# Spreading eight heads' attention tasks over a calendar, float32 sums of squares, one more weight sum by accumulating DMA, and padding tiles, in a one-core encoder layer

## The chip, the cores and the metric

One core of a Trainium2 chip runs the whole kernel as one program. The metric is the device time of one execution in microseconds (us). TensorE (PE) multiplies, VectorE (DVE), ScalarE (ACT) and GpSimd (POOL) do elementwise work, SyncE (SP) and POOL issue DMAs.

## The reference

One residual layer over 512 frames of width 2048. A combined projection gives q, k, v (8 heads of 128), u and v_sgu (1024 each) and two gates (2048 each). Attention is stick-breaking: no softmax, strictly causal.

```python
h = rms_norm(x, g_mix)
q, k, v_sb, u, v_sg, gate_a, gate_b = jnp.split(h @ w_in, splits, axis=-1)
q, k = rms_norm(q, g_q), rms_norm(k, g_k)                    # per head
z = einsum('bhtd,bhsd->bhts', q, k) * 128 ** -0.5
log_keep = where(past, log_sigmoid(-z), 0)
a = where(past, exp(log_sigmoid(z) + tail_sum(log_keep)), 0) # tail: over later s < t
y_a = (a @ v_sb) @ w_oa
y_b = (gelu(u) * (W_s LN(gelu(v_sg)) + b)) @ w_ob            # W_s: 8 groups, 128 x 128
x = x + (sigmoid(gate_a) * y_a + sigmoid(gate_b) * y_b) @ w_out
x = x + square(relu(rms_norm(x, g_ff) @ w_ff1)) @ w_ff2
```

## The kernel before

**Numbers.** Matrix operands are held as two float32r parts, `hi` and `lo` (hi by an ACT cast, lo by a DVE subtraction, `split_to`, L106 to L112), and a product is the sum of two or three float32r matmuls over the parts (`mm3`, L72 to L74).

**Stages.** v and v_sgu are projected by tokens (`by_token`). Then comes the stage that the change touches: a list `order` of 28 *pairs* of 128-column blocks of `w_in` (20 gate pairs, 8 head pairs, where a head's pair is its q and k). Then the projections `ya`, `yb`, `xo`, the hidden layer in pairs too (`w_ff1`), and the last product (`w_ff2`).

**A pair.** `strassen_pair` computes one pair in seven products (Strassen's scheme in Winograd's form) in the sequence `TREE = ("y11", "m7", "m6", "y21", "m5", "m4", "y22")`. PE does 16 matmuls for each (L221 with `hi`, L224 with `lo`; m7 has 24 by `mm3`). Several products run on in one PSUM bank, the *trunk* (named `q`), and after y11, m6 and m5 ACT copies the trunk into another bank (`fork`, L229), from which y21, m4 and y22 go on. The weights of a product are sums of four loaded blocks w11, w12, w21, w22, 512 KB each: `Sums.parts` makes the sum and splits it. In `parts`, "m7" is w11 + w21 (DVE, L181); "m5" is w21 + w22, done by a DMA that POOL issues with `accum_op=ALU.add` (L183); "m6" adds w22 to the m7 sum in the tile `c` (DVE, L185); "y22" adds w12 to `c` (DVE, L187).

**Attention tasks.** When a head's pair is done, `attend(h, act)` returns 18 small tasks, which are put into the queue `behind`; `step()`, called after every product, takes one task from it. A task only records instructions behind that product's. The tasks are, in this order: `square` of q, `of_q`, `square` of k, `of_k`, nothing, `scaled_k`, nothing, `weigh(3)`, `weigh(2)`, `weigh(1)`, `weigh(0)`, `fetch_v`, nothing, `turn(0)`, `turn(1)`, `turn(2)` with `turn(3)`, nothing, `product`. So they fill 18 of the 21 products from one head's pair to the next (`order` has two gate pairs between heads).
- `square` (L525) squares q or k on ACT and splits the squares into hi and lo. `factors` (L532) sums them over the head's 128 dimensions: eight float32r matmuls of 4 columns into `ms`; POOL raises that to the power -1/2 (`r`, L537).
- `of_k` makes two diagonal matrices `dg` of k's factors by eight ACT instructions (L552); `scaled_k` multiplies them by ones on PE (`rows`, L558) and scales k.
- `weigh(tb)` is one block row of the attention: scores `z` on PE, two sigmoids on ACT (`keep` L579, `beta` L580), a masking and a running product on DVE (L581, L584), a masking on POOL (L587), and the product `beta` on DVE (L588).
- `turn(sb)` transposes the finished weights on PE (`aT`, L597) and splits them; `product` multiplies them by v into `o`.

**What sets the order.** The code is recorded in the order above, and then each engine's instruction stream is arranged by the framework's own estimate of times; on the chip each engine goes through its stream strictly in that order, and waits where an operand isn't there.

Of the kernel before, what the change touches and what calls it, by code (L numbers as in the profile page):

```python
# [16 lines left out]
P = 128  # L17
# [18 lines left out]
def tile_hybrid_layer(ctx: ExitStack, tc: tile.TileContext, x, g_mix, w_in, g_q, g_k, ln_g, ln_b,  # L36
# [39 lines left out]
    state = {"load": None, "raw": raws}  # L76
    behind = collections.deque()

    def step():
        if behind:  # L80
            behind.popleft()()

    def flush():
        while behind:
            step()

    def weight(wap, kt, c0, w=W):
# [75 lines left out]
    class Sums:  # L163


        def __init__(self, blocks, tiles, loaded=True):


            self.blocks, self.loaded = blocks, loaded
            self.w11, self.w12, self.w21, self.w22, self.a, self.c = tiles  # L170
            self.take = {"y11": self.w11, "y21": self.w12, "m7": self.a, "m6": self.c, "y22": self.c,
                         "m4": self.w22, "m5": self.w21}
# [6 lines left out]
        def parts(self, name):  # L179
            if name == "m7":  # L180
                nc.vector.tensor_tensor(out=self.a, in0=self.w11, in1=self.w21, op=ALU.add)  # L181
                if self.loaded:
                    state["sum"] = nc.gpsimd.dma_start(out=self.w21, in_=self.blocks[1, 1], accum_op=ALU.add)  # L183
            if name == "m6":
                nc.vector.tensor_tensor(out=self.c, in0=self.a, in1=self.w22, op=ALU.add)  # L185
            if name == "y22":
                nc.vector.tensor_tensor(out=self.c, in0=self.c, in1=self.w12, op=ALU.add)  # L187
            if name == "m5" and not self.loaded:
                nc.vector.tensor_tensor(out=self.w21, in0=self.w21, in1=self.w22, op=ALU.add)
            src = self.take[name]  # L190
            hi, lo = piece("w_hi"), piece("w_lo")
            like = "p (k c) -> p k c"
            hi, lo = (t.rearrange(like, k=src.shape[1]) for t in (hi, lo))
            split_to(hi, lo, src)
            return hi, lo

    def column_sums(wap, c0, loaded=True):

        KH = KT // 2
        c0 = c0 if isinstance(c0, tuple) else (c0, c0 + P)  # L200
        blocks = {(h, c): wap[:, c0[c]:c0[c] + P].rearrange("(k h p) c -> h p k c", p=P, h=2)[h]
                  for h in range(2) for c in range(2)}
        w = Sums(blocks, [state["raw"].tile([P, KH, P], F32, name="w_raw", tag="w_raw") for _ in range(6)],
                 loaded)
        collections.deque(w.loads(), 0)
        return w

# [64 lines left out]
        def __getitem__(self, k):  # L272
            return self.ys[self.name, k]

    def strassen_pair(wap, c0, ys, forks, loaded=True, ready=None):
# [11 lines left out]
        w, first = ready or (column_sums(wap, c0, loaded), None)  # L287
        strassen_columns(w, {name: Late(ys, name) for name in NAMES}, forks, evac, first)
        return act

# [71 lines left out]
    mhalf = const.tile([P, 4], F32, name="mhalf")  # L362
    nc.gpsimd.memset(mhalf, -0.5)

    minus_one = const.tile([P, 4], F32, name="minus_one")
    nc.gpsimd.memset(minus_one, -1.0)
    ones_r = const.tile([P, P], F32R, name="ones_r")
# [146 lines left out]
    def attend(h, act):  # L514
# [5 lines left out]
        def small4(name, dt=F32):  # L520
            return small.tile([P, NTB], dt, name=name, tag=name, bufs=3)

        def square(src):
            t = slot("sq")
            nc.scalar.activation(out=t, in_=src, func=AF.Square)  # L525
            part["sq"] = split(t, "sq")

        def factors():
            m = acc("ms")
            for tb in range(NTB):  # L530
                for i, sq in enumerate(part["sq"]):
                    nc.tensor.matmul(m[:, tb * 4:tb * 4 + 4], lhsT=sq[:, tb * P:(tb + 1) * P], rhs=ones_r[:, :4],  # L532
                                     start=i == 0, stop=i == 1)
            t, f = small4("ms"), small4("r")
            nc.vector.tensor_tensor(out=t, in0=m[:, :16].rearrange("p (b r) -> p b r", r=4)[:, :, 0], in1=eps_x,
                                    op=ALU.add)
            nc.gpsimd.tensor_tensor(out=f, in0=t, in1=mhalf, op=ALU.pow)  # L537
            return f

        def of_q():  # L540
            r[1], r[-1] = factors(), small4("nr")
            nc.gpsimd.tensor_tensor(out=r[-1], in0=r[1], in1=minus_one, op=ALU.mult)
            part["q"] = split(q, "qT")

        def of_k():
            f, f_hi, f_lo = factors(), small4("r_hi", F32R), small4("r_lo")
            nc.vector.tensor_copy(out=f_hi, in_=f)
            nc.vector.tensor_tensor(out=f_lo, in0=f, in1=f32(f_hi), op=ALU.subtract)
            part["dg"] = [slot("dg", F32R) for _ in range(2)]
            for t, x in zip(part["dg"], (f32(f_hi), f_lo)):  # L550
                for tb in range(NTB):
                    nc.scalar.activation(out=t[:, tb * P:(tb + 1) * P], in_=ident, func=AF.Copy,  # L552
                                         scale=x[:, tb:tb + 1])

        def scaled_k():
            rows = acc("rows")
# [47 lines left out]
        def product():  # L604
# [3 lines left out]
            for i, x in enumerate(split(o, "oT")):  # L608
                nc.sync.dma_start(out=held_o[h, i], in_=f32(x))

        return [lambda: square(q), of_q, lambda: square(k), of_k, lambda: None, scaled_k, lambda: None,
                lambda: weigh(3), lambda: weigh(2), lambda: weigh(1), lambda: weigh(0), fetch_v, lambda: None,
                lambda: turn(0), lambda: turn(1), lambda: (turn(2), turn(3)), lambda: None, product]

    wsT, ws, bs = [], [], []
    held_s = dram.tile([6, P, W], F32, name="held_s")
# [83 lines left out]
    opened = []  # L700

    def open_gates():
        w = column_sums(win, US)
        opened.append((w, w.parts(TREE[0])))

    for half in range(2):
# [24 lines left out]

    gate_pairs = [(US + n * P, n, AF.Gelu) for n in range(0, SGW // P, 2)]
    gate_pairs += [(GA + n * P, SGW // P + n, AF.Sigmoid) for n in range(0, 2 * D // P, 2)]
    order = gate_pairs[:2]
    for h in range(HEADS):
        order += [h] + gate_pairs[2 * h + 2:2 * h + 4]
    order += gate_pairs[2 * HEADS + 2:]
    behind.append(moments)
    forks = new_forks(hy["y11", 0])
    oT = []  # L740
# [4 lines left out]
    for i, item in enumerate(order):  # L745
        if i == len(order) - 1:
            with tc.issue_after(state["sum"].ins):
                for h in range(2):
                    fetch_o(h, slots)
        if isinstance(item, int):  # L750
            behind.extend(attend(item, strassen_pair(win, (item * P, SBW + item * P), hy, forks)))
        else:
            c0, n, func = item
            gated(n, strassen_pair(win, c0, hy, forks, ready=opened.pop() if opened else None), func)

    with tc.issue_after(state["sum"].ins):
        for h in range(2, HEADS):
# [333 lines left out]
```

## Time and profile before

| | |
|---|---|
| median of 3 runs | 2515.2 us (2514.13 to 2515.55) |
| the profiled execution | 2515.11 us, of which its span is 2513.4 us |
| PE busy | 2460.3 us of the span |
| DVE, ACT, POOL busy | 1908.5, 1278.4, 434.5 us |
| HBM traffic | 383.29 MB read, 89.65 MB written |

Matmuls overlap in the rows: a 128x512 matmul is shown with 395 ns, and the next begins about 233 ns after it, so the number that counts is the distance between starts. PEclk is the granted clock of TensorE as a share of full speed. In the stage with the 28 pairs (about 180 to 870 us of the span) the tasks of the heads lie between the products.

### The profile page before, as it was taken

How to read it: one execution, taken by the hardware profiler on the slowest of the kernel's cores; microseconds unless marked ns; L12 is line 12 of the kernel's file. 1: busy time of each engine (PE TensorE's matmuls, PEld its weight loads, DVE VectorE, ACT ScalarE, POOL GpSimd, SP SyncE). 2: the span in 40 equal slices, each digit the busy share in tenths (PEclk: the TensorE clock that was granted, in tenths of full speed). 3: DMA queues.
4: the chain of work that ended last, by engine and by line, in shares of the span. 5: the costliest groups of instructions: out<-in, count | busy, mean ns of one | idle time of the engine just before them, and what ended most of it. 6: DMA issues, size and time to landing. Idle time of an engine off the chain costs nothing.

```text
span 2513.4 us, 35343 instructions
## 1 busy us (share of the span) xinstructions
PE 2460.3 (98%) x12920; PEld 2090.3 (83%) x12920; DVE 1908.5 (76%) x2541; ACT 1278.4 (51%) x1931; POOL 434.5 (17%) x556
## 2 busy tenths in 40 slices
PE   9999899999999999999999999999999999999999
PEld 7788788888888878888898888888888878888887
DVE  4567777777777755533689888888888998888887
ACT  5235565655655422322467777767665443333333
POOL 0101120212121332300000000000014334322210
PEclk9999999999999999999999999999999999999999
DMA  5555556555554863433469988888886999866753
GB/s 181 189 150 151 126 130 149 132 137 140 132 137 126 257 227 126 152 126 126 117 160 244 225 235 221 227 230 222 232 273 237 289 306 301 248 213 198 236 173 96
DMA packets 482653, 476.31 MB, mean 190 GB/s; under 512 B 20208, under 2 KB 372528, under 8 KB 482480
## 3 DMA queue, kind: packets, MB, share of 16 engines
q1 hardware_dynamic: 385232, 336.68, 42.2%
q0 software_dynamic: 96960, 136.87, 24.2%
q8 instruction: 101, 1.65, 0.3%
q10 hardware_dynamic: 288, 0.52, 0.1%
q14 instruction: 72, 0.59, 0.1%
HBM read 383.29 MB, written 89.65 MB: 188 GB/s over the span
## 4 chain that ended last, share of the span: by engine, by line
PE 61%; DVE 1%; DMA 0%; issue 0%; ACT 0%; ACTq 0%; DVEq 0%
PE q L72 9%; PE q L73 9%; PE q L74 9%; PE fork L221 7%; PE q L221 7%; PE fork L224 4%; PE q L224 4%; PE xo L74 2%; PE xo L72 2%; PE xo L73 2%; PE yb L73 1%; PE yb L74 1%; PE yb L72 1%; DMA store<-ys 0%; PE f L72 0%; PE f L73 0%
## 5 line engine op out<-in xcount | busy, mean ns | idle before, releaser
L108 ACT CAST w_hi<-w_raw 128x1024 fp32r<-128x1024 f32 (+1 forms) x639 | 669.3, 1048 | 719.8 <-PE q L73 338.4
L109 DVE TENSOR_TENSOR w_lo<-w_raw,w_hi 128x1024 fp32r<-128x1024 f32 (+1 forms) x639 | 780.3, 1222 | 245.9 <-ACT w_hi L108 230.2
L73 PE MATMUL q<-w_lo,ys 128*128 128x512 f32 x896 | 353.9, 395 | 0.7 <-DVE w_lo L109 0.7
L74 PE MATMUL q<-w_hi,ys 128*128 128x512 f32 x896 | 353.8, 395 | 0.0
L221 PE MATMUL q<-ys,w_hi 128*128 128x512 f32 x1192 | 311.1, 398 | 11.3 <-ACT fork L229 11.3
L72 PE MATMUL q<-w_hi,ys 128*128 128x512 f32 x896 | 318.5, 396 | 0.6 <-ACT w_hi L108 0.5
L221 PEld LDWEIGHTS q<-ys,w_hi 128*128 128x128 f32 x1192 | 210.5, 188 | 50.3 <-ACT fork L229 13.0
L221 PE MATMUL fork<-ys,w_hi 128*128 128x512 f32 x968 | 245.6, 395 | 0.0
L183 POOL DMA_DIRECT2D w_raw<-in_w_ff_dram x58 | 80.9, 1394 | 915.0 <-ACT act L282 325.7
L96 DVE TENSOR_TENSOR w_lo<-w_raw,w_hi 128x1024 fp32r<-128x1024 f32 x99 | 124.7, 1259 | 144.4 <-ACT w_hi L94 144.2
L94 ACT CAST w_hi<-w_raw 128x1024 fp32r<-128x1024 f32 x99 | 103.7, 1048 | 238.7 <-issue 84.5
L221 PEld LDWEIGHTS fork<-ys,w_hi 128*128 128x128 f32 x968 | 175.4, 188 | 35.5
L73 PEld LDWEIGHTS q<-w_lo,ys 128*128 128x128 f32 x896 | 167.9, 187 | 42.9 <-DVE w_lo L109 1.5
L72 PEld LDWEIGHTS q<-w_hi,ys 128*128 128x128 f32 x896 | 167.8, 187 | 42.0 <-ACT w_hi L108 0.9
L74 PEld LDWEIGHTS q<-w_hi,ys 128*128 128x128 f32 x896 | 168.1, 188 | 40.9
L224 PEld LDWEIGHTS q<-ys,w_lo 128*128 128x128 f32 x1192 | 162.5, 188 | 13.4
L224 PE MATMUL q<-ys,w_lo 128*128 128x256 f32 x1192 | 165.8, 281 | 0.0
L990 POOL DMA_DIRECT2D ys<-store x224 | 126.1, 588 | 186.0 <-PE q L74 118.6
L224 PEld LDWEIGHTS fork<-ys,w_lo 128*128 128x128 f32 x968 | 131.9, 189 | 11.0
L1033 DVE SCALAR_TENSOR_TENSOR total<-q,plus,total 128x512 f32<-128x512 f32 x180 | 132.5, 744 | 6.6 <-PE q L74 4.8
L224 PE MATMUL fork<-ys,w_lo 128*128 128x256 f32 x968 | 134.2, 281 | 0.0
L72 PE MATMUL q<-ys,w_hi 128*128 128x256 f32 x472 | 133.2, 282 | 0.0
(270 smaller groups left out, 4566.5 us busy)
## 6 DMA issues: line engine op xcount, KB each, us to landing
w_raw<-in_w_ff_dram SPq DMA_DIRECT2D x256, 512.0 KB, 5.6
w_raw<-in_w_in_dram SPq DMA_DIRECT2D x143, 512.0 KB, 4.2
ys<-store POOLq DMA_DIRECT2D x224, 256.0 KB, 6.2
w_raw<-in_w_ff_dram POOLq DMA_DIRECT2D x58, 512.0 KB, 6.7
store<-ys_hi SPq DMA_DIRECT2D x90, 256.0 KB, 4.2
store<-ys_lo SPq DMA_DIRECT2D x90, 256.0 KB, 5.5
w_raw<-in_w_out_dram SPq DMA_DIRECT2D x32, 512.0 KB, 4.0
w_raw<-in_w_in_dram POOLq DMA_DIRECT2D x28, 512.0 KB, 6.3
```

Of the source, the lines that this page charges most:

```text
L72: nc.tensor.matmul(o, lhsT=lh[0], rhs=rh[0], start=start, stop=False, **kw)
L73: nc.tensor.matmul(o, lhsT=lh[0], rhs=rh[1], start=False, stop=False, **kw)
L74: nc.tensor.matmul(o, lhsT=lh[1], rhs=rh[0], start=False, stop=stop, **kw)
L94: nc.scalar.copy(out=hi, in_=raw)
L96: nc.vector.tensor_tensor(out=lo, in0=raw, in1=f32(hi), op=ALU.subtract)
L108: nc.scalar.copy(out=hi, in_=src)
L109: state["lo"] = nc.vector.tensor_tensor(out=lo, in0=src, in1=f32(hi), op=ALU.subtract)
L183: state["sum"] = nc.gpsimd.dma_start(out=self.w21, in_=self.blocks[1, 1], accum_op=ALU.add)
L221: nc.tensor.matmul(o, lhsT=hi[:, k, :], rhs=rhs[name][k], start=name == "y11" and k == 0, stop=False, skip_group_check=True)
L224: nc.tensor.matmul(o[:, :HS], lhsT=lo[:, k, :], rhs=rhs[name][k][:, :HS], start=False, stop=k == KH - 1, skip_group_check=True)
L990: nc.gpsimd.dma_start(out=f32(t), in_=store[f][HELD.index(name), p])
L1033: nc.vector.scalar_tensor_tensor(out=a, in0=o, scalar=part, in1=a, op0=ALU.mult, op1=ALU.add)
```

## The change

1. `attend` no longer returns a list. It puts its tasks into a `calendar`, each at a fixed number of steps after the head's pair: 1, 2, 4, 5, 7, 8, 10, 13, 15, 17, 19, 24, 25, 26 and 30, where before it took 18 steps in a row. `of_k`'s diagonals become two tasks of their own. The next head comes after 21 steps, so a head's last tasks stand among the next head's first.
2. The squares are not split any more: four float32 matmuls instead of eight float32r ones add them up.
3. In the 28 pairs of this stage (`twice=True`) the sum for y22 is made by a second accumulating DMA, issued by POOL behind the split for m6, instead of by DVE.
4. Two tiles of 32 bytes that nothing uses are added, in the pools `const` and `small`. In the built program the 2048-byte slots then begin at a multiple of 128 bytes (before: 64 bytes past one) and the weight pieces too (before: 96 bytes past one).
5. The first head follows the first gate pair instead of the second.

```diff
+    calendar, now = collections.defaultdict(list), [0]
     def step():
         if behind:
             behind.popleft()()
+        for task in calendar.pop(now[0], ()):
+            task()
+        now[0] += 1
...
-            if name == "y22":
+            if name == "y22" and not self.twice:
                 nc.vector.tensor_tensor(out=self.c, in0=self.c, in1=self.w12, op=ALU.add)
...
             split_to(hi, lo, src)
+            if name == "m6" and self.twice:
+                state["sum"] = nc.gpsimd.dma_start(out=self.c, in_=self.blocks[1, 0], accum_op=ALU.add)
...
+    const.tile([P, 8], F32, name="even")
+    small.tile([P, 8], F32, name="even", tag="even", bufs=1)
...
-        def square(src):
-            t = slot("sq")
-            nc.scalar.activation(out=t, in_=src, func=AF.Square)
-            part["sq"] = split(t, "sq")
+        def square(src, name):
+            part[name] = slot("sq")
+            nc.scalar.activation(out=part[name], in_=src, func=AF.Square)
-        def factors():
+        def factors(name):
             m = acc("ms")
             for tb in range(NTB):
-                for i, sq in enumerate(part["sq"]):
-                    nc.tensor.matmul(m[:, tb * 4:tb * 4 + 4], lhsT=sq[:, tb * P:(tb + 1) * P], rhs=ones_r[:, :4],
-                                     start=i == 0, stop=i == 1)
+                nc.tensor.matmul(m[:, tb * 4:tb * 4 + 4], lhsT=part[name][:, tb * P:(tb + 1) * P], rhs=ones[:, :4],
+                                 start=True, stop=True)
...
-        return [lambda: square(q), of_q, lambda: square(k), of_k, lambda: None, scaled_k, lambda: None,
-                lambda: weigh(3), lambda: weigh(2), lambda: weigh(1), lambda: weigh(0), fetch_v, lambda: None,
-                lambda: turn(0), lambda: turn(1), lambda: (turn(2), turn(3)), lambda: None, product]
+        tasks = {1: lambda: square(q, "sq_q"), 2: lambda: square(k, "sq_k"), 4: of_q, 5: of_k,
+                 7: lambda: diagonal(0), 8: lambda: diagonal(1), 10: scaled_k, 13: lambda: weigh(3),
+                 15: lambda: weigh(2), 17: lambda: weigh(1), 19: lambda: (weigh(0), fetch_v()),
+                 24: lambda: turn(0), 25: lambda: turn(1), 26: lambda: (turn(2), turn(3)), 30: product}
+        for n, task in tasks.items():
+            calendar[now[0] + n].append(task)
...
-    order = gate_pairs[:2]
+    order = gate_pairs[:1]
     for h in range(HEADS):
-        order += [h] + gate_pairs[2 * h + 2:2 * h + 4]
+        order += [h] + gate_pairs[2 * h + 1:2 * h + 3]
```

How this moves instructions is shown at three places. The first is PE's stream from the last scores `z` of a head to its first transposes `aT`. Before, from the second head:

```order
L74 MATMUL z<-kT_hi,qT_lo 128x128
L221 MATMUL q<-ys,w_hi 128x512 x4
L224 MATMUL q<-ys,w_lo 128x256 x8
L221 MATMUL fork<-ys,w_hi 128x512 x8
L224 MATMUL fork<-ys,w_lo 128x256 x8
L221 MATMUL fork<-hT,w_hi 128x512 x8
L224 MATMUL fork<-hT,w_lo 128x256 x8
L597 MATMUL aT<-ident,beta 128x128 x4
```

After, the same place (line numbers are those of the changed file; behind the last row but one stand the 24 matmuls of an m7):

```order
L74 MATMUL z<-kT_hi,qT_lo 128x128
L228 MATMUL q<-ys,w_hi 128x512 x8
L231 MATMUL q<-ys,w_lo 128x256 x8
L228 MATMUL fork<-ys,w_hi 128x512 x8
L231 MATMUL fork<-ys,w_lo 128x256 x8
L228 MATMUL q<-hT,w_hi 128x512 x6
L228 MATMUL fork<-hT,w_hi 128x512 x8
L231 MATMUL fork<-hT,w_lo 128x256 x8
L228 MATMUL q<-hT,w_hi 128x512 x2
L231 MATMUL q<-hT,w_lo 128x256 x8
...
L607 MATMUL aT<-ident,beta 128x128 x2
```

Between the two stood two and three quarter products, and now there are five.

The second place is PE's stream where `rows` stood: the end of y11 in the trunk (`q<-hT`), and the m6 that goes on in the same bank (`q<-ys`, 512 wide). Before:

```order
L558 MATMUL rows<-dg,ones_r 128x512
L224 MATMUL fork<-hT,w_lo 128x256 x8
L224 MATMUL q<-hT,w_lo 128x256 x4
L221 MATMUL q<-ys,w_hi 128x512 x8
L224 MATMUL q<-ys,w_lo 128x256 x8
```

After, the same pair of a head's period (an m7 of 24 matmuls, of which the first is shown, stands between):

```order
L228 MATMUL q<-hT,w_hi 128x512 x3
L228 MATMUL fork<-hT,w_hi 128x512 x8
L231 MATMUL fork<-hT,w_lo 128x256 x8
L228 MATMUL q<-hT,w_hi 128x512 x5
L231 MATMUL q<-hT,w_lo 128x256 x8
L72 MATMUL q<-ys,w_hi 128x256
...
L228 MATMUL q<-ys,w_hi 128x512 x8
L231 MATMUL q<-ys,w_lo 128x256 x8
```

Before, m6 followed y11 at once, once for every head; in the changed stream a y11 is never followed at once by its m6.

The third place is POOL's stream over about one head. Before (L183 is the DMA for m5):

```order
L183 DMA w_raw<-in_w_in_dram 128x8x128 x2
L537 TENSOR_TENSOR r<-ms,mhalf 128x4 x2
L542 TENSOR_TENSOR nr<-r,minus_one 128x4
L587 TENSOR_TENSOR beta<-beta,past 128x128 x3
L183 DMA w_raw<-in_w_in_dram 128x8x128
L587 TENSOR_TENSOR beta<-beta,past 128x128
L566 DMA v<-held_a 128x4x128 x2
```

After (L188 is the DMA for m5, L201 the new one for y22):

```order
L201 DMA w_raw<-in_w_in_dram 128x8x128
L188 DMA w_raw<-in_w_in_dram 128x8x128
L544 TENSOR_TENSOR r<-ms,mhalf 128x4
L549 TENSOR_TENSOR nr<-r,minus_one 128x4
L544 TENSOR_TENSOR r<-ms,mhalf 128x4
L201 DMA w_raw<-in_w_in_dram 128x8x128
L188 DMA w_raw<-in_w_in_dram 128x8x128
L597 TENSOR_TENSOR beta<-beta,past 128x128
L201 DMA w_raw<-in_w_in_dram 128x8x128
L597 TENSOR_TENSOR beta<-beta,past 128x128
L188 DMA w_raw<-in_w_in_dram 128x8x128
```

The small operations of a head now stand between twice as many DMAs.

More of the change, by code (lines that the diff above doesn't have):

```diff
@@ L81, in step @@
             behind.popleft()()
+        for task in calendar.pop(now[0], ()):
+            task()
+        now[0] += 1
     def flush():
-        while behind:
+        while behind or calendar:
             step()
@@ L163, in tile_hybrid_layer, with __init__ @@
     class Sums:
-        def __init__(self, blocks, tiles, loaded=True):
-            self.blocks, self.loaded = blocks, loaded
+        def __init__(self, blocks, tiles, loaded=True, twice=False):
+            self.blocks, self.loaded, self.twice = blocks, loaded, twice
             self.w11, self.w12, self.w21, self.w22, self.a, self.c = tiles
@@ L194, in parts, with column_sums @@
             split_to(hi, lo, src)
+            if name == "m6" and self.twice:
+                state["sum"] = nc.gpsimd.dma_start(out=self.c, in_=self.blocks[1, 0], accum_op=ALU.add)
             return hi, lo
-    def column_sums(wap, c0, loaded=True):
+    def column_sums(wap, c0, loaded=True, twice=False):
         KH = KT // 2
@@ L203, in column_sums @@
         w = Sums(blocks, [state["raw"].tile([P, KH, P], F32, name="w_raw", tag="w_raw") for _ in range(6)],
-                 loaded)
+                 loaded, twice)
         collections.deque(w.loads(), 0)
@@ L273, in __getitem__, with strassen_pair @@
             return self.ys[self.name, k]
-    def strassen_pair(wap, c0, ys, forks, loaded=True, ready=None):
+    def strassen_pair(wap, c0, ys, forks, loaded=True, ready=None, twice=False):
         act = [slot("act"), slot("act")]
@@ L285, in evac @@
                 state["evac"] = nc.vector.tensor_tensor(out=a, in0=a, in1=side, op=ALU.add)
-        w, first = ready or (column_sums(wap, c0, loaded), None)
+        w, first = ready or (column_sums(wap, c0, loaded, twice), None)
         strassen_columns(w, {name: Late(ys, name) for name in NAMES}, forks, evac, first)
@@ L540, in of_q @@
         def of_q():
-            r[1], r[-1] = factors(), small4("nr")
+            r[1], r[-1] = factors("sq_q"), small4("nr")
             nc.gpsimd.tensor_tensor(out=r[-1], in0=r[1], in1=minus_one, op=ALU.mult)
@@ L545, in of_k, with diagonal @@
         def of_k():
-            f, f_hi, f_lo = factors(), small4("r_hi", F32R), small4("r_lo")
+            f, f_hi, f_lo = factors("sq_k"), small4("r_hi", F32R), small4("r_lo")
             nc.vector.tensor_copy(out=f_hi, in_=f)
             nc.vector.tensor_tensor(out=f_lo, in0=f, in1=f32(f_hi), op=ALU.subtract)
[L549 to L553, printed above, removed]
+            part["f"], part["dg"] = [f32(f_hi), f_lo], []
+        def diagonal(i):
+            t = slot("dg", F32R)
+            for tb in range(NTB):
+                nc.scalar.activation(out=t[:, tb * P:(tb + 1) * P], in_=ident, func=AF.Copy,
+                                     scale=part["f"][i][:, tb:tb + 1])
+            part["dg"].append(t)
         def scaled_k():
@@ L702, in open_gates @@
     def open_gates():
-        w = column_sums(win, US)
+        w = column_sums(win, US, twice=True)
         opened.append((w, w.parts(TREE[0])))
@@ L733, in tile_hybrid_layer @@
     gate_pairs += [(GA + n * P, SGW // P + n, AF.Sigmoid) for n in range(0, 2 * D // P, 2)]
-    order = gate_pairs[:2]
+    order = gate_pairs[:1]
     for h in range(HEADS):
-        order += [h] + gate_pairs[2 * h + 2:2 * h + 4]
-    order += gate_pairs[2 * HEADS + 2:]
+        order += [h] + gate_pairs[2 * h + 1:2 * h + 3]
+    order += gate_pairs[2 * HEADS + 1:]
     behind.append(moments)
@@ L750, in tile_hybrid_layer @@
         if isinstance(item, int):
-            behind.extend(attend(item, strassen_pair(win, (item * P, SBW + item * P), hy, forks)))
+            attend(item, strassen_pair(win, (item * P, SBW + item * P), hy, forks, twice=True))
         else:
             c0, n, func = item
-            gated(n, strassen_pair(win, c0, hy, forks, ready=opened.pop() if opened else None), func)
+            gated(n, strassen_pair(win, c0, hy, forks, ready=opened.pop() if opened else None, twice=True),
+                  func)
     with tc.issue_after(state["sum"].ins):
```

## Prediction

> **What bounds the kernel.** I read the page first, then PE's table of waits, then timelines at those waits, then the granted clock behind them.
>
> ```profile
> PE 2460.3 (98%) x12920; PEld 2090.3 (83%) x12920; DVE 1908.5 (76%) x2541; ACT 1278.4 (51%) x1931; POOL 434.5 (17%) x556
> ```
>
> PE is the bound: 2460.3 of 2513.4 us, 53.1 idle. No change to DVE, ACT, POOL or DMA is worth anything unless PE waits for it. Where it does is told by PE's waits (us in total, times, longest):
>
> ```profile
> PE aT L597 <- DVE beta L588: 32.6, 8, 5.2
> PE q L221 <- ACT fork L229: 11.3, 8, 1.4
> PE ya L72 <- DVE merged_a L825: 1.6, 2, 1.3
> ```
>
> Two waits, each once per head, are 43.9 of the 53.1 us. The first, at the second head, in PE's timeline and then in DVE's (start, duration, what, in brackets the idle time before and its releaser):
>
> ```profile
> 371.24 0.27 PE L74 MATMUL z<-kT_hi,qT_lo 128*128 128x128 f32 x1
> 377.95 1.11 PE L224 MATMUL fork<-hT,w_lo 128*128 128x256 f32 x8
> 382.98 1.11 PE L597 MATMUL aT<-ident,beta 128*128 128x128 f32 x4 [3.91 <-DVE beta L588]
> ```
> ```profile
> 371.34 1.22 DVE L181 TENSOR_TENSOR w_raw<-w_raw 128x1024 f32<-128x1024 f32 x1
> 372.48 1.21 DVE L584 TENSOR_TENSOR_SCAN rest<-keep 128x384 f32<-128x384 f32 x1
> 377.94 0.68 DVE L584 TENSOR_TENSOR_SCAN rest<-keep 128x256 f32<-128x256 f32 x1
> ...
> 380.19 0.41 DVE L588 TENSOR_TENSOR beta<-beta,rest 128x255 f32<-128x255 f32 x1
> ...
> 382.64 0.28 DVE L588 TENSOR_TENSOR beta<-beta,rest 128x127 f32<-128x127 f32 x1
> ```
>
> The last scores were done at 371.5; DVE then worked through a queue of four block rows, mixed with weight sums and splits, and gave the last `beta` at 382.9. PE had 7.6 us of other work and stood 3.9. The second wait:
>
> ```profile
> 358.40 1.05 ACT L108 CAST w_hi<-w_raw 128x1024 fp32r<-128x1024 f32 x1
> 359.35 0.59 ACT L229 COPY fork<-q 128x512 f32<-128x512 f32 x1
> ```
> ```profile
> 357.93 0.64 PE L224 MATMUL q<-hT,w_lo 128*128 128x256 f32 x4
> 359.99 0.73 PE L221 MATMUL q<-ys,w_hi 128*128 128x512 f32 x2 [1.42 <-ACT fork L229]
> ```
>
> Here m6 followed y11 in the same bank at once, and PE waited for the copy, which stood behind a weight cast.
>
> **The clock behind the first wait.** Windows of 8 us that begin when each `aT` wait has ended (columns: PE, PEld, DVE, ACT, POOL busy, granted clock, DMA share, GB/s):
>
> ```profile
> 308.10:316.10 8.00, 7.99 (x37) 7.22 (x38) 5.11 (x8) 3.94 (x5) 0.00 (x0) 0.62 0.12 31
> 383.00:391.00 8.00, 8.00 (x50) 7.44 (x51) 5.63 (x9) 3.68 (x7) 0.00 (x0) 0.82 0.28 86
> 456.40:464.40 8.00, 8.00 (x47) 7.36 (x48) 5.57 (x9) 3.73 (x6) 0.00 (x0) 0.79 0.34 109
> 530.10:538.10 8.00, 8.00 (x38) 7.23 (x39) 5.53 (x9) 3.77 (x6) 0.00 (x0) 0.63 0.29 96
> 604.90:612.90 8.00, 8.00 (x50) 7.44 (x51) 5.63 (x9) 3.68 (x7) 0.00 (x0) 0.82 0.29 89
> 678.30:686.30 8.00, 8.00 (x47) 7.37 (x48) 5.56 (x9) 3.83 (x6) 0.00 (x0) 0.79 0.34 107
> 752.00:760.00 8.00, 8.00 (x38) 7.23 (x39) 5.31 (x9) 3.65 (x6) 0.00 (x0) 0.63 0.19 60
> 826.80:834.80 8.00, 8.00 (x51) 7.44 (x51) 5.54 (x9) 3.86 (x7) 0.00 (x0) 0.83 0.38 117
> 360.00:368.00 8.00, 8.00 (x51) 7.31 (x52) 4.63 (x7) 3.98 (x7) 0.10 (x1) 1.00 0.55 162
> ```
>
> PE is shown as fully busy, and yet ran at 0.62 to 0.83 of its clock. What was lost is (1 - clock) times 8 us: shares of 0.38, 0.18, 0.21, 0.37, 0.18, 0.21, 0.37 and 0.17, together 2.07, or 16.6 us. The last row begins after a 1.42 us wait: clock 1.00, nothing lost. So a short wait costs itself, and one of 3.9 us half as much again.
>
> **The change part by part.**
>
> *The calendar, first wait.* In PE's new stream five products, with the m7 among them, stand between the last `z` and the first `aT`. A product lasts 2.81 us, by the chain's starts of two neighbours:
>
> ```profile
> 1293.94 1.87 PE q L221 x8
> 1296.75 1.87 PE fork L221 x8
> ```
>
> That is 14.0 us of cover for the chain that took 11.4 us (371.5 to 382.9). And the chain itself shrinks: `weigh(3)` and `weigh(2)` come two or three products earlier than `weigh(1)`, and of the DVE work between, only what stands before the last `beta` counts. In the new DVE stream nine instructions stand between `keep` of `weigh(1)` and the last `beta`, three of 1.2 us and six of 0.3 to 0.7 by the rows above, some 6 us. I take the wait as gone: -32.6; it would return only if DVE ran 5 us or more behind. With it goes the lost clock: -16.6.
>
> *The calendar, second wait.* In the new stream a y11 is never followed by its m6 without an m7 (2.8 us) between, and the copy came 1.4 us late. -11.3.
>
> *What is late next.* In the new stream `rows` stands behind `ms` of k at a distance of half a product, one product (2.8), an m7 (2.8) and an `o` (1.9), in all about 8.9 us. Before, this chain was shown by:
>
> ```profile
> 346.50 0.25 PE L532 MATMUL ms<-ones_r,sq_lo 128*128 128x4 f32 x1
> 350.00 1.28 ACT L552 ACTIVATE dg<-ident,r_hi 128x128 fp32r<-128x128 f32 x4 [0.18 <-DVE r_hi L547]
> 351.70 1.27 ACT L552 ACTIVATE dg<-ident,r_lo 128x128 fp32r<-128x128 f32 x4
> ```
>
> 6.2 us from 346.75 to 352.97. A gate's sigmoid and an evacuation stand ahead of it on ACT now, about 1 us more: 7.3 of 8.9. A wait of 0 to 1 us per head is possible: 0 to 8 us. I take 2, since the sum of the chain lies under the cover.
>
> *Squares in float32.* Removed on ACT and DVE are 16 casts and 16 subtractions of `sq`; PE never waited for either, so nothing. On PE, eight matmuls become four of float32. The trace has float32 matmuls in `along` (four in the code):
>
> ```profile
> L467 PE MATMUL rp<-dg,ones x8: 271/275/275, 71.9 to 72.7; 128*128 128x128 f32 x8
> 345.83 0.25 PE L532 MATMUL ms<-ones_r,sq_lo 128*128 128x4 f32 x1
> ```
>
> Four matmuls leave eight rows, that is two passes each, 0.11 us apart (0.8 us over seven steps); the old `ms` rows are 0.11 apart too (345.83 to 346.50 over six). So 128 passes before and 128 after: 0. Bounds: if a pass of 4 columns cost half or twice as much, -7 or +14.
>
> The Trainium skill, in "FP8 and Floating Point Precision", section "TensorE Precision Notes", says that true FP32 takes four passes through the array. By that it would be 256 passes instead of 128. The rows above show two passes per matmul, and the sum goes by them.
>
> *The sum for y22 by DMA.* Removed on DVE: 28 additions of 1.22 us, 34 us of an engine that PE waits for only at `aT`; nothing beside the wait already counted. Added on POOL: 28 DMAs like those for m5:
>
> ```profile
> L183 POOL DMA_DIRECT2D w_raw<-in_w_in_dram x28: 1540/1588/1641, 180.7 to 841.2; - x28
> DMA to landing us min/median/max: 5.5/6.6/10.2
> L187 DVE TENSOR_TENSOR w_raw<-w_raw x91: 1207/1219/1227, 201.2 to 2480.9; 128x1024 f32<-128x1024 f32 x91
> ```
>
> 28 x 1.59 = 44 us on POOL, which is busy 17%. What counts is the landing: the cast and split for y22, on ACT and DVE, now wait for it, and with them everything behind on these queues (fork copies, evacuations, sigmoids). y22's split comes four products (11.2 us) after m6's; the median landing is 6.6, the worst 10.2, and behind an m5 DMA that was issued a product earlier about 6.6 + 6.6 - 2.8 = 10.4. The m5 DMA has only three products (8.4 us), its worst landing of 10.2 is over that, and yet no wait of PE for a weight stands in this stage: 1.8 us of lateness are absorbed. So 0; the upper end is in the rivals. HBM reads grow by 28 blocks of 512 KB, in a stage where the DMA share is 0.55. Behind these DMAs on POOL stand `r` and `beta`; a 1.6 us issue ahead of `r` was there before (it is in the 6.2 us chain).
>
> *Alignment.* The streamed operand lay 64 bytes (slots) or 96 bytes (weight pieces) past a multiple of 128. The chain's rows above stream slots: 1.87 / 8 = 0.234 us. In `w_ff2` the weights stream:
>
> ```profile
> 1904.23 0.39 PE L72 MATMUL q<-w_hi,ys 128*128 128x512 f32 x1
> 1904.46 0.40 PE L73 MATMUL q<-w_lo,ys 128*128 128x512 f32 x1
> 1904.70 0.39 PE L74 MATMUL q<-w_hi,ys 128*128 128x512 f32 x1
> ```
>
> 0.23 and 0.24 us between starts: the same at both offsets. No row has offset 0, so this isn't excluded, but where 64 and 96 make no difference I take 0.
>
> *One gate pair moved behind the first head; the last fetches behind one more DMA.* The stage's work is the same. The fetches of `oT` for `ya` stand behind a last DMA of 1.6 us; PE's only wait in `ya` is 1.6 us in two. 0, at most +3.
>
> **Sum.** The profiled execution took 2515.11 us, 1.7 more than its span, and 0.1 below the median of the runs (2515.2). 2515.1 - 32.6 - 11.3 - 16.6 + 2 = 2456.6; I say 2457, that is 2.3% less. As a check by another way: a head's period is (826.8 - 383.0) / 6 = 74.0 us, from the begins of the second and the last but one row of the windows; its three pairs are 3 x 7 products, 59.1 us, and the head's own matmuls about 7. That leaves 7.9 us per head or 63 in eight, against my 60.5.
>
> **Rivals.**
>
> *The y22 DMA comes late (slower).* For: two DMAs per pair now share a queue, and ACT and DVE stand in order behind them. Against: 10.4 of 11.2 us, and 1.8 more absorbed. Price: each us of lateness above that, in 28 pairs, is 28 us of waiting. At 1 us: 2485. The gain is gone when PE waits 60.5 / 28 = 2.2 us per pair, that is when the DMAs land after 11.2 + 1.8 + 2.2 = 15.2 us; above that it is slower, and above a wait of 3.9 us the clock adds half as much again.
>
> *A wait moves (half the gain).* `rows`, `aT` or `z` turn out late by 2 us for each head, without loss of clock: 2454.6 + 16 = 2471. If one of them reaches 3.9 us, half as much again: 2454.6 + 8 x 6 = 2502. For: the estimate that arranged the streams was wrong by 4 us at `aT` before. Against: covers of 14 and 8.9 us for chains of about 8 and 7.3.
>
> *Alignment speeds up PE.* The Trainium skill, in "TensorE: Matmul & The Clock Gate", section "Back-to-back issue gap", gives N/2.4 + 2.5 ns, 216 ns for 512 columns; the rows have 233. No page says that alignment is the difference. As a mechanism of this kernel: a row of 2048 bytes touches 17 lines of 128 bytes where an aligned one touches 16. If the stream's rate went by lines, the 2444 us of PE work (2460.3 - 16.6) would fall by 1/17, 144 us, and the time to about 2313. Only the equal rates at 64 and 96 speak against it.
>
> *Float32 takes four passes.* 128 more passes of 0.11 us: +14, 2471. For it speaks only the page named above; against it the eight rows of `rp`.
>
> *Only the lost clock and the first wait go* (the second wait returns elsewhere): 2466.
>
> **How the numbers follow.** My forecast, both waits and the clock gone and at most 8 us of new waits (2452 to 2464): 0.70. A wait moves, or the second stays (2464 to 2502): 0.14. The DMA late: 0.10, of which 0.03 slower than before. Alignment: 0.04. Four passes: 0.02. The range is 2448 to 2485: it holds the forecast, the moved waits up to 4 us a head and a DMA 1 us late in each pair, and leaves out the alignment case and the worst of the others, together under 2 in 10. 0.2% (5 us) is about what this kernel's runs can tell from no change; faster 0.95, same 0.02, slower 0.03.
>
> **What would show it.** Right: no row `aT <- DVE beta` and none `q <- ACT fork` in PE's waits; granted clock 1.00 in every window of the stage; PE idle about 10 us; `ms` as 128 rows; PE starts 0.233 us apart as before. Wrong: a wait of PE for `w_hi` of y22 or of ACT for a DMA of `w_raw` (first rival); a wait at `rows` or `z` (second); starts below 0.23 us (third).

## The result and the profile after

The changed kernel takes 2417.3 us (median of 4 runs, 2416.6 to 2418.9), against 2515.4 of the kernel before in the same job: a ratio of 0.9612, with an interval of 0.9595 to 0.9628. The prediction was 2457, with a range from 2448 to 2485. So 98 us went where 58 were expected.

First PE's line on the page, then PE's table of waits, then a window over the stage of the 28 pairs (columns as in the prediction):

```profile
PE 2406.2 (100%) x12920; PEld 2081.5 (86%) x12920; DVE 1860.8 (77%) x2497; ACT 1272.7 (53%) x1917; POOL 473.4 (20%) x584
```
```profile
PE ya L72 <- DVE merged_a L839: 1.7, 2, 1.3
PE idle L359 <- POOL ones L355: 1.2, 1, 1.2
PE q L73 <- DVE w_lo L114: 1.0, 3, 0.5
```
```profile
180.00:840.00 660.00, 659.38 (x4011) 590.76 (x4010) 490.77 (x683) 399.82 (x655) 182.41 (x187) 1.00 0.85 192
```

The rows for `aT` and for the fork copy are gone, the granted clock is 1.00 over the stage, and PE is idle for 9.8 us of its 2416.0 us span. So far this is what was forecast. What was not forecast stands in PE's timeline in `w_ff2`, where the weights are the moving operand of a matmul (the one that is streamed, `rhs` in the code; the other, `lhsT`, is the stationary one), and in the chain of work, where slots are:

```profile
1904.23 0.39 PE L73 MATMUL q<-w_lo,ys 128*128 128x512 f32 x1
1904.46 0.39 PE L74 MATMUL q<-w_hi,ys 128*128 128x512 f32 x1
1904.69 0.39 PE L73 MATMUL q<-w_lo,ys 128*128 128x512 f32 x1
1904.91 0.39 PE L74 MATMUL q<-w_hi,ys 128*128 128x512 f32 x1
1905.14 0.39 PE L72 MATMUL q<-w_hi,ys 128*128 128x512 f32 x1
```
```profile
1199.15 1.84 PE fork L228 x8
1201.94 1.84 PE q L228 x8
```

The starts are 227.5 ns apart (0.91 us over four steps) instead of 0.23 to 0.24 us, and eight matmuls of 512 columns take 1.84 instead of 1.87 us in the chain.

All versions of the kernel, each against the kernel before in its own job (2513.8 to 2515.7); two more kernels, probe and probe_w, carry series of matmuls behind their end and stand in their own paragraphs. Of w32_s32 one of two executions was disturbed (granted clock 0.75) and is left out here, so it has a single time and no interval.

| kernel | us | ratio, interval |
|---|---|---|
| the changed kernel | 2417.3 | 0.9612, 0.9595 to 0.9628 |
| no_align: changed, without the padding tiles | 2452.7 | 0.9754, 0.9739 to 0.9769 |
| align_alone: before, with the padding tiles | 2479.6 | 0.9864, 0.9849 to 0.9880 |
| calendar_alone: before, with calendar and order | 2450.1 | 0.9747, 0.9730 to 0.9765 |
| no_calendar: before, with float32 squares and y22 by DMA | 2473.0 | 0.9837, 0.9822 to 0.9853 |
| w0_s96: changed, weight pieces at 0, slots at 96 | 2453.4 | 0.9754, 0.9725 to 0.9782 |
| w96_s0: changed, weight pieces at 96, slots at 0 | 2446.7 | 0.9727, 0.9699 to 0.9755 |
| w32_s32: changed, both at 32 | 2422.6 | one run |
| m7_wide: changed, m7 in 512 columns | 2413.2 | 0.9604, 0.9591 to 0.9617 |
| lo_0: m7_wide in longer tiles | 2412.6 | 0.9592, 0.9579 to 0.9605 |
| lo_past: lo_0, lo pieces of the pairs 208 bytes on | 2403.8 | 0.9556, 0.9543 to 0.9569 |

### The profile page after: what moved, and what is told of

It is laid out like the page before. It is cut to its first block, busy times and chain, and to the rows that moved or that the text cites. A ratio compares the mean times of both kernels' runs of the same rounds, so it can differ in the third digit from the quotient of the medians.

```text
span 2416.0 us, 35273 instructions
## 1 busy us (share of the span) xinstructions
PE 2406.2 (100%) x12920; PEld 2081.5 (86%) x12920; DVE 1860.8 (77%) x2497; ACT 1272.7 (53%) x1917; POOL 473.4 (20%) x584
## 3 DMA queue, kind: packets, MB, share of 16 engines
q8 instruction: 101, 1.65, 0.3%
## 4 chain that ended last, share of the span: by engine, by line
PE 61%; DVE 2%; issue 1%; DMA 0%; ACT 0%; DVEq 0%
PE q L73 9%; PE q L74 9%; PE q L72 9%; PE q L228 7%; PE fork L228 7%; PE q L231 4%; PE fork L231 4%; PE xo L74 2%; PE xo L72 2%; PE xo L73 2%; PE yb L72 1%; PE yb L73 1%; PE yb L74 1%; DVE w_lo L114 1%; DMA w_raw<-in_w_ff_dram 0%
## 5 line engine op out<-in xcount | busy, mean ns | idle before, releaser
L74 PE MATMUL q<-w_hi,ys 128*128 128x512 f32 x896 | 348.6, 389 | 0.0
L72 PE MATMUL q<-w_hi,ys 128*128 128x512 f32 x896 | 312.5, 389 | 0.8 <-ACT w_hi L113 0.6
L228 PE MATMUL q<-ys,w_hi 128*128 128x512 f32 x1192 | 305.5, 394 | 0.0
L188 POOL DMA_DIRECT2D w_raw<-in_w_ff_dram x58 | 81.0, 1396 | 900.9 <-ACT act L289 444.4
L186 DVE TENSOR_TENSOR w_raw<-w_raw 128x1024 f32<-128x1024 f32 x91 | 111.2, 1223 | 32.1 <-DMA w_raw<-in_w_in_dram 20.3
```

What stands on the lines that cost most here:

```text
L72: nc.tensor.matmul(o, lhsT=lh[0], rhs=rh[0], start=start, stop=False, **kw)
L74: nc.tensor.matmul(o, lhsT=lh[1], rhs=rh[0], start=False, stop=stop, **kw)
L228: nc.tensor.matmul(o, lhsT=hi[:, k, :], rhs=rhs[name][k], start=name == "y11" and k == 0, stop=False, skip_group_check=True)
```

## Experiments

**Which part brought what.** Four kernels, in one job. Theory A: the padding does what the forecast lacks. The rival: the calendar brings more than the waits.

no_align takes the two padding tiles out of the changed kernel (as shown), and align_alone puts them into the kernel before:

```diff
-    const.tile([P, 8], F32, name="even")
-    small.tile([P, 8], F32, name="even", tag="even", bufs=1)
```

no_align: 

> The changed kernel without the two padding tiles. Theory A: 0.233 us apart, no wait of PE at aT or fork, and the time that was predicted for the change, 2455 to 2458. Theory B: 0.227 us apart and 2417. Theory C: 2440 to 2455.

align_alone: 

> The kernel before with the two padding tiles alone (slots and weight pieces at 0 past a multiple of 128 bytes). Theory A (the alignment of what PE reads sets the rate of its stream): starts of 512-column matmuls 0.227 us apart instead of 0.233, both kinds of waits as before (aT 32 us, fork 11 us), and the time falls by what the prediction missed, 40 us: 2475. Theory B (the rate follows from the lighter DVE, the moved DMAs or the unbroken stream, not from the addresses): 0.233 us apart and 2515. Theory C (padding only helps together with the calendar): between, 2500.

Measured: 2452.7 and 2479.6. The kernel before took 2514.4 in this job: the padding alone brings 35 us, all the rest 62, together 97, and 98 were measured in one. In align_alone PE's waits are those of before, and the clock is 0.97 over the stage as it was before:

```profile
PE aT L599 <- DVE beta L590: 33.0, 8, 5.2
PE q L221 <- ACT fork L229: 11.6, 8, 1.7
```
```profile
180.00:840.00 660.00, 615.34 (x3700) 550.26 (x3699) 501.26 (x684) 383.06 (x637) 123.26 (x111) 0.97 0.57 137
```

So the padding touches neither of the two waits: it speeds up PE's own stream. Averaged over the starts in unbroken sequences of the traces, a 512-column matmul that streams weights takes 233.3 ns from start to start in no_align and 227.0 in the changed kernel (4,140 steps: -26 us), one that streams slots 233.4 and 229.6 (3,628 steps: -14), and a 256-column one 118.6 and 119.5 (4,519 steps: +4). That makes -36, and the times differ by 35. The mean of the slots lies above that of the weights because the pace needs some matmuls to settle: by their place in an unbroken run of 512-column matmuls on slots, the first five steps take 229 to 235 ns in the changed kernel, and from the sixth on it is 227.

calendar_alone takes the calendar and the order of the pairs, and keeps the split squares, y22 on DVE and the old addresses (part of its edit is shown); no_calendar is the opposite without the padding (the old queue of 18 steps and the old order, with float32 squares and y22 by DMA):

```diff
# calendar_alone, against the changed kernel
-            part[name] = slot("sq")
+            t = slot("sq")
...
+            part[name] = split(t, "sq")
...
-        w = column_sums(win, US, twice=True)
+        w = column_sums(win, US)
```

calendar_alone: 

> The kernel before with the calendar (and the heads one gate pair earlier) alone: squares split, y22 sums on DVE, no padding. If the calendar alone takes both waits and the lost clock: 2455 to 2458, no wait at aT. If the lighter DVE is needed as well: an aT wait of 1 to 3 us per head stays, 2465 to 2490.

no_calendar: 

> The kernel before with the float32 squares and the y22 sums by DMA alone: old queue of tasks, no padding. If the waits come from the order of the tasks: aT waits of about 3.9 us and the slow clock behind them stay, 2505 to 2515. If they come from DVE's load (34 us of sums and 11 us of splits less): the aT wait falls under 2.5 us, no slow clock, 2470 to 2490.

Measured: 2450.1 and 2473.0. In calendar_alone both waits are gone; in no_calendar the first is halved, the second gone, and the clock falls behind one of the eight waits that are left. PE's waits of calendar_alone (the two longest), then three rows of no_calendar's:

```profile
PE ya L72 <- DVE merged_a L838: 1.6, 2, 1.3
PE idle L359 <- POOL ones L355: 1.2, 1, 1.2
```
```profile
PE aT L607 <- DVE beta L598: 15.3, 8, 3.0
PE ya L72 <- DVE merged_a L836: 1.6, 2, 1.3
PE rows L568 <- ACT dg L561: 1.1, 1, 1.1
```

Two of no_calendar's waits, the longest (3.02 us) and the last (1.82 us), in PE's timeline, and windows of 8 us behind each of them:

```profile
303.61 0.66 PE L607 MATMUL aT<-ident,beta 128*128 128x128 f32 x4 [3.02 <-DVE beta L598]
782.84 0.77 PE L607 MATMUL aT<-ident,beta 128*128 128x128 f32 x4 [1.82 <-DVE beta L598]
```
```profile
303.60:311.60 8.00, 7.99 (x56) 7.43 (x57) 5.64 (x10) 6.00 (x9) 1.59 (x1) 1.00 0.78 143
782.80:790.80 8.00, 7.96 (x47) 7.24 (x48) 5.70 (x9) 3.59 (x6) 1.59 (x1) 0.79 0.89 168
```

The calendar alone (with its order of the pairs, which no run separates from it) brings 64 us. The relief of DVE and ACT alone brings 41: 17.3 at `aT`, 11.3 at the fork, the 16.6 of the clock but for the 1.7 lost behind the last wait (0.21 of 8 us), less 1.1 at `rows`, 42 by these rows. How much of it is the squares' and how much the y22 sum's was not tried. Both remedies remove the same waits, so together they bring 62, not 105. The `aT` wait of 3.0 us and six of 1.7 to 1.8 cost no clock here, and one of 1.8 did, so its length alone does not tell which wait will.

**What the padding does.** Theories on operands: the moving one sets the rate (M), the stationary one (S), both must be aligned (B), or they must only lie alike (R). A series measures it by itself; three paddings test it in the kernel. The profiles show no addresses: where an operand begins is known from the built program, and in the series from their code.

```diff
+    for m, s, n in combos:
+        o = aux(...)
+        for j in range(40):
+            a = s + j % 6 * P
+            b = m + j % 2 * 448
+            nc.tensor.matmul(o[:, :n], lhsT=still[:, a:a + P], rhs=moving[:, b:b + n], ...)
```

probe: 

> The changed kernel with 23 series of 40 float32r matmuls behind its end, on PE alone. The name of a series tells how far past a multiple of 128 bytes its operands begin (m: the moving one, w: the stationary one; a is 0, c 32, e 64, g 96 bytes) and how many columns it streams (x 512, y 256, z 384). The kernel's own 512-column matmuls settle at 227 ns between starts where both operands begin at 0, and at 233.4 where the kernel before had them at 64 and 96; 256 columns take 120 and 118. Theory M (the moving operand alone sets it): series with m at a take 227 ns whatever w is, all others 233. Theory S (the stationary one alone, that is the load): w at a takes 227, all others 233. Theory B (both must be aligned): only ma with wa takes 227. Theory R (they must only lie alike): aa, cc, ee and gg take 227, the other twelve 233. By the lines of 128 bytes that a row touches (my rival case of alignment) m at 0 would take 16/17 of the others, 219.7 against 233.4. For 256 columns I expect the reverse, 120 where the 512-column series is fast and 118 elsewhere. At 128 and at 16 bytes (i, b) M says that i is as a, and b as c. The series add some 200 us at the end, so the time is about 2617 us.

Picked rows of PE's timeline over the series (start, duration of all forty; a fortieth of the way to the next start is the pace; the letter behind `m` tells where the moving operand begins, that behind `w` where the stationary one does):

```profile
2415.29 9.23 PE L1096 MATMUL probemawax<-probe_m,probe_w 128*128 128x512 f32 x40
2424.36 9.50 PE L1096 MATMUL probemcwax<-probe_m,probe_w 128*128 128x512 f32 x40
2433.70 9.33 PE L1096 MATMUL probemewax<-probe_m,probe_w 128*128 128x512 f32 x40
2452.19 9.49 PE L1096 MATMUL probemawcx<-probe_m,probe_w 128*128 128x512 f32 x40
2461.51 9.23 PE L1096 MATMUL probemcwcx<-probe_m,probe_w 128*128 128x512 f32 x40
2507.75 9.23 PE L1096 MATMUL probemewex<-probe_m,probe_w 128*128 128x512 f32 x40
2516.82 9.50 PE L1096 MATMUL probemgwex<-probe_m,probe_w 128*128 128x512 f32 x40
2544.86 9.49 PE L1096 MATMUL probemewgx<-probe_m,probe_w 128*128 128x512 f32 x40
2554.19 9.26 PE L1096 MATMUL probemgwgx<-probe_m,probe_w 128*128 128x512 f32 x40
2563.29 4.95 PE L1096 MATMUL probemaway<-probe_m,probe_w 128*128 128x256 f32 x40
2568.08 4.87 PE L1096 MATMUL probemeway<-probe_m,probe_w 128*128 128x256 f32 x40
2614.73 9.49 PE L1096 MATMUL probembwbx<-probe_m,probe_w 128*128 128x512 f32 x40
```

Both at 0: (2424.36 - 2415.29) / 40 = 226.8 ns; only the stationary one at 0, the moving one at 32: (2433.70 - 2424.36) / 40 = 233.5. Both at 32, or at 64, or at 96, is as fast as both at 0 (9.23 to 9.26 us). Of the twelve unlike pairs ten take 233 to 234 ns, and two (the moving operand 64 bytes further on) 229. The two pairs of the kernel before, 64 with 96 and 96 with 64, are among the slow ones (`gwe` and `ewg`, 9.50 and 9.49 us). Theory R holds but for the two at 229, and M, S and B fall. With 256 columns the like pairs are the slower ones here: 120 against 118 ns. One row speaks against the plain form of R: with both at 16 bytes (last row) the series is slow. And the time was 2627, ten above what I had said.

w0_s96: 

> The changed kernel with other padding: the weight pieces begin at 0 and the slots at 96 bytes past a multiple of 128. In the stages by tokens (and xo) the weight pieces are the moving operand, 4224 matmuls of 512 columns; in the pairs, ya and yb the slots are, 3600 of 512 and 4440 of 256 columns. In the two runs on the padding a 512-column matmul gained 5.3 ns in the mean and a 256-column one lost 1.3. Theory M (moving): only the token stages gain, 22 us of the 2452.7 without padding: 2431, with 227 ns in w_ff2 and 233 in the pairs. Theory S (stationary): only the pairs, ya and yb gain, 13 us: 2440, with 233 in w_ff2 and 227 in the pairs. Theory B (both) and theory R (lying alike): 2453.

w96_s0: 

> The opposite: weight pieces at 96, slots at 0. Theory M: the pairs, ya and yb gain, 13 us: 2440. Theory S: the token stages gain, 22 us: 2431. Theories B and R: 2453.

w32_s32: 

> Both at 32 bytes past a multiple of 128. Theories M, S and B: 2453, as without padding. Theory R (they must only lie alike): 2417, as the changed kernel.

Their edits are the sizes of the two tiles: w0_s96 has 32 bytes in `const` and none in `small`, w96_s0 none and 64, w32_s32 64 and 32. That of w32_s32, against the changed kernel:

```diff
-    const.tile([P, 8], F32, name="even")
+    const.tile([P, 16], F32, name="even")
     small.tile([P, 8], F32, name="even", tag="even", bufs=1)
```

Measured: 2453.4, 2446.7 and 2422.6. PE's window in `w_ff2` for the three, in this order (the number behind PE's busy time is that of its matmuls in 50 us):

```profile
1900.00:1950.00 50.00, 50.00 (x216) 40.15 (x216) 45.87 (x56) 20.72 (x23) 16.55 (x29) 1.00 0.88 295
```
```profile
1900.00:1950.00 50.00, 50.00 (x216) 40.29 (x215) 46.53 (x54) 20.18 (x24) 14.15 (x25) 1.00 0.88 287
```
```profile
1900.00:1950.00 50.00, 50.00 (x222) 41.44 (x221) 45.09 (x58) 22.26 (x28) 10.72 (x16) 1.00 0.86 285
```

216 matmuls where only one of the two is at 0, 222 where both lie alike and neither is: R again. w96_s0 is 6 us better than R said. Its 512-column matmuls take 233.5 and 233.3 ns as without padding; its 256-column ones take 117.3 instead of 118.6, which is the 6 us over 4,519.

w32_s32 has the paces of the changed kernel (227.0, 229.6 and 119.5 ns) and yet 5 us more. Part of it is a wait in `ya` that the changed kernel's trace does not have, and the clock behind it. PE's timeline, then a window behind the wait:

```profile
822.30 0.33 PE L806 MATMUL mix<-wsp,vn_lo 128*128 128x128 f32 x1 [0.48 <-DVE vn_lo L114]
823.88 0.58 PE L73 MATMUL ya<-oT,w_hi 128*128 128x512 f32 x1 [1.25 <-DMA oT<-held_o]
```
```profile
824.20:827.50 3.30, 3.30 (x9) 2.59 (x8) 0.00 (x0) 0.00 (x0) 0.46 (x1) 0.50 1.04 387
```

1.25 us of wait, and 3.3 us at half the clock, 1.65 lost: 2.9 of the 5. PE's other waits add up to 7.5 us in its table where the changed kernel's are 5.5, which makes 4.9 in all. This is one execution of each; that the padding has no part in these waits is not shown.

**A finer series, and versions that use it.** probe_w keeps the moving operand at 0 and moves the stationary one in steps of 16 bytes over 256, alone and in the kernel's own sequence of 8 x 512 and 8 x 256 columns.

probe_w: 

> The changed kernel with 48 series behind its end in which the moving operand begins at 0 and the stationary one at 0, 16, 32 ... 240 bytes past a multiple of 256 of it (letters a to p): 512 columns (x), 256 columns (y), and 8 of 512 with both at 0 followed by 8 of 256 with the stationary one at the offset, twice (z). Theory R (512 columns take 226.7 ns only where both lie alike, here modulo 256, since the series with 0 and 128 took 232): x at a 226.7, all others 229 to 235, and i (128 bytes) 232. For 256 columns 120 at a and at most 118 elsewhere; w96_s0, with a distance of 96 bytes, had 117.0 in the mean. If R holds only modulo 128, i is 226.7 too. The series take about 230 us.

The kernel with these series took 2641.7 us. Picked rows of PE's timeline (x are 512 columns, y 256, z the sequence; a is 0 bytes, b 16, c 32, e 64, i 128, n 208, p 240):

```profile
2414.93 5.60 PE L1093 MATMUL probexa<-probe_m,probe_w 128*128 128x512 f32 x24
2420.37 5.61 PE L1093 MATMUL probexb<-probe_m,probe_w 128*128 128x512 f32 x24
2425.82 5.75 PE L1093 MATMUL probexc<-probe_m,probe_w 128*128 128x512 f32 x24
2459.37 5.76 PE L1093 MATMUL probexi<-probe_m,probe_w 128*128 128x512 f32 x24
2498.38 5.62 PE L1093 MATMUL probexp<-probe_m,probe_w 128*128 128x512 f32 x24
2503.84 3.03 PE L1093 MATMUL probeya<-probe_m,probe_w 128*128 128x256 f32 x24
2515.22 2.89 PE L1093 MATMUL probeye<-probe_m,probe_w 128*128 128x256 f32 x24
2549.22 5.76 PE L1093 MATMUL probeza<-probe_m,probe_w 128*128 128x512 f32 x32
2621.79 5.68 PE L1093 MATMUL probezn<-probe_m,probe_w 128*128 128x512 f32 x32
```

For 512 columns 0, 16 and 240 bytes settle at 226.7 ns (240 after the first few), 128 (i) takes 233.3: with the moving operand at 0, what counts is the distance modulo 256, and there is one fast place, 16 bytes to either side. I had expected 16 and 240 to be slow. For 256 columns, 64 bytes give 113.3 and 0 gives 120.0, but so do 112 and 128, which the expectation had at 118 or less; and in the kernel's sequence 64 gives 117.5, and 208 is the best. From the begin of a z series to the next one's (2627.31 and 2554.81) it is 5.52 us at 208 and 5.59 at 0.

m7_wide writes the product m7 as the others are written, so that 8 matmuls of 512 and 8 of 256 columns take the place of 24 of 256:

```diff
-            o = side[:, :HS] if name == "m7" else ...
-            if name == "m7":
-                for k in range(KH):
-                    mm3(o, (hi[:, k, :], lo[:, k, :]), sides(rhs[name][k]), ...)
+            o = side if name == "m7" else ...
...
+            if name == "m7":
+                both = slot("m7")[:, :HS]
+                nc.scalar.copy(out=both, in_=side[:, :HS])
+                nc.vector.tensor_tensor(out=both, in0=both, in1=side[:, HS:], op=ALU.add)
```

m7_wide: 

> The changed kernel, with m7 written as the other six products are: 8 matmuls of 512 columns with hi and 8 of 256 with lo, instead of 24 of 256; ACT copies one half of the bank and DVE adds the other, once per pair. Operands that lie alike take 227 ns for 512 columns and 120 for 256 (the probe): 347 instead of 360 ns for each of 472 steps, 6 us: 2411. If, as in the kernel before, 512 took 233 and 256 took 117 to 118, it would be 350 instead of 352: 2416, no change. If the added ACT and DVE work is waited for, above 2417.

Measured 2413.2 (2411.5 to 2417.4): 4 us less, and the two intervals overlap. PE's line shows 472 matmuls less, and 5.4 us less of busy time:

```profile
PE 2400.8 (100%) x12448; PEld 2056.2 (85%) x12448; DVE 1885.8 (78%) x2556; ACT 1279.0 (53%) x1976; POOL 478.3 (20%) x584
```

lo_past shifts the lo pieces of the pairs by 208 bytes (52 words); lo_0 has the same tiles and no shift:

```diff
-            hi, lo = piece("w_hi"), piece("w_lo")
+            hi, lo = piece("w_hi"), piece("w_lo", 52 if src.shape[1] == KT // 2 else 0)
```

lo_past: 

> m7_wide, with the lo pieces of the pairs' weights 208 bytes further on in tiles that are 256 bytes longer (the hi pieces, and lo in the stages by tokens, lie alike with the slots as before; a small tile is taken from the slots to make room). In the series of 8 x 512 and 8 x 256 columns the starts took 5403 ns in all with the lo pieces at 208 and 5474 with them at 0, 35 ns less for each product. A pair has seven products and there are 59 pairs: 413 x 35 ns = 14.7 us, 2398 to 2399. If only the 256-column matmuls gain (116.5 instead of 119.9 ns in the same series) and not the 512-column ones ahead of them: 413 x 8 x 3.4 ns = 11 us, 2402. If the offset of lo means nothing in the kernel, 2413.

lo_0: 

> The same kernel, longer tiles and all, with the lo pieces at 0, so that only the offset differs from lo_past. Expected as m7_wide, 2413; what it differs from that comes from the tiles and the order, not from the offset.

Measured 2403.8 and 2412.6: the offset alone brings 8.8 us, and the intervals do not meet. The chain of lo_past, then of lo_0 (eight 512-column matmuls each; the distance of two rows is a product):

```profile
1208.87 1.83 PE q L226 x8
1211.63 1.83 PE q L226 x8
```
```profile
1211.03 1.84 PE q L226 x8
1213.82 1.84 PE q L226 x8
```

A product takes 2.76 instead of 2.79 us. Over all, the 256-column matmuls went from 119.2 to 117.3 ns (3,574: -7.0 us) and the 512-column ones that stream slots from 229.7 to 228.7 (4,100: -4.0). That is 11 us by the trace, and less than the 14.7 of the series. The 512-column matmuls, whose own operands did not move, gain because they settle sooner: the third to fifth step of a run take 227 to 228 ns instead of 229 to 232. In the profiled run a wait for `oT` of 1.07 us in `ya`, again right behind one of 0.48, and half the clock for 3.4 us took some 2.8 of that back. At 2403.8 us this is the best version, 0.6% below the changed kernel.

## Why the prediction was wrong

**The step that failed** is the alignment, taken as 0: "0.23 and 0.24 us between starts: the same at both offsets". It measured 35 us, alone (2514.4 to 2479.6) and beside the rest (2452.7 to 2417.3). The rows were right and the conclusion was not. I asked where the streamed operand lay, and compared 64 with 96. But where slots streamed from 64, weight pieces stood still at 96, and where pieces streamed from 96, slots stood still at 64: in both rows the operands lay unlike, so two rows that looked like two cases were one. What the padding changed is that both now begin alike, and the runs show that this sets the pace. The prediction said that no row had offset 0, and then took the value of the rows instead of keeping both ends in the range.

**The third rival** had the right part and the wrong size: 16 lines instead of 17 would be 219.7 ns for 512 columns, and it is 227; and the 256-column matmuls became slower, by 0.9 ns. It also named the wrong cause: operands at 32 or 96 bytes are as fast, if they lie alike. Its sign, starts below 0.23 us, came all the same. The 216 ns that the Trainium skill ("TensorE: Matmul & The Clock Gate", section "Back-to-back issue gap") gives for a matmul by itself were reached by no float32r series here: the fastest took 226.7.

**The waits and the clock**, 32.6 + 11.3 + 16.6 = 60.5: right. no_align is 62 and calendar_alone 64 below the kernel before, with both rows gone and the clock at 1.00. That the 16.6 comes with the wait is shown by align_alone, which kept both (0.97 over the stage), and by the kernels without the wait, which have neither. "A short wait costs itself, and one of 3.9 us half as much again" holds as a mean only. In the prediction's own rows equal waits of 3.9 us are followed by 0.82 and by 0.63, and in no_calendar one of 1.8 us cost 1.7 where one of 3.0 cost nothing. Without the alignment the forecast of 2457 was 4 us off.

**What is late next**, +2 at `rows`: not needed, since PE's waits of the changed kernel have no such row. Why no_align and calendar_alone lie 2 and 4.5 us below 2454.6 stays open: PE's busy time is 2440.0 and 2439.8 us in them, some 4 below 2460.3 - 16.6.

**Float32 squares**, 0 on PE: right. The `ms` matmuls of the changed kernel:

```profile
L539 PE MATMUL ms<-ones,sq x128: 171/252/253, 243.8 to 712.6; 128*128 128x4 f32 x128
```

These are 128 rows for 64 matmuls, two for each. The Trainium skill ("FP8 and Floating Point Precision", section "TensorE Precision Notes") says four passes; the rows show two, as `rp` did before, and whether one holds more than one pass they do not tell. For the time it does not matter: the 128 rows of before were `hi` and `lo`, and their starts are 0.11 us apart as those of after.

**The y22 sum by DMA**, 0: right for PE. What waited most for this DMA in the changed kernel (us, times), and when it landed:

```profile
  ACT w_hi L113: 42.4, 17
DMA to landing us min/median/max: 6.1/8.3/9.5
```

The landing stayed under the 10.4 us that the prediction allowed. ACT stood 42.4 us behind 17 of the 28, at most 3.7 at a time, and PE waited for none of them. So one sign that the prediction named for the first rival came, a wait of ACT for a DMA of `w_raw`, and it cost nothing: only a wait of PE would have told. The first rival (it lands too late for PE) did not come; neither did the second (a wait moves) nor the one on four passes. What DVE and ACT gained is worth 41 us where the calendar is not there, and nothing on top of it: no_align, with these two parts, is 2.6 us above calendar_alone, and the two intervals overlap.

## What to carry to other kernels

Where PE is the bound at full clock, look at the distance between its starts, and at where both operands of a matmul begin: compare the address of the stationary operand with that of the moving one, modulo 256 bytes, before a rate is called fixed. Two rows are two cases only if they differ in what is asked for, and where no row has the asked value, both ends belong in the range. Two remedies for one wait do not add up, while a remedy for waits and one for the rate do.

## What the runs showed of the hardware

- The pace of float32r matmuls with a new stationary operand each depends on how far apart the two operands begin, modulo 256 bytes. For 512 columns it is 226.7 ns at a distance of 0, and of 16 with the moving one at 0; 229 to 230 where the moving one is 64 or 80 further on; and 232 to 234 elsewhere. For 256 columns the order is another: in series of their own 120.0 ns at 0, and at 112 and 128 too, 113.3 with the stationary one 64 on, and 116.7 to 119.8 elsewhere.
- A moving operand that begins 16 bytes past a multiple of 32 is slow at both distances that were tried, 16 (231.5 ns) and 0 (233), so the distance is not all. Why any of this is so the runs do not show; in what order PE reads its two operands was not tried.
- The pace needs some matmuls to settle. In the changed kernel, where the operands lie alike, the first five steps of a run of 512-column matmuls on slots take 229 to 235 ns, and the later ones 227.
- The granted clock fell to 0.50 for some 3.4 us (382.5 to 385.8 us of the kernel before) or for twice that (307.4 to 314.1), and not in proportion to the wait. Behind waits of 3.9 us it was one or the other; behind no_calendar's it did not fall after 3.0 us nor after six of 1.7 to 1.8, and fell for 3.4 us after one of 1.8. It also came behind two short waits that follow each other: 0.48 and then 1.25 us, which ended 1.6 us apart, were followed by 3.3 us at 0.50.
